# A written instruction order for the seven-product projections, and a later S5 gate, in a four-branch encoder layer

## The chip, the cores and the metric

One NeuronCore of a Trainium2 chip runs the whole kernel as one program. The metric is device microseconds of one execution. A NeuronCore has four compute engines with a queue each, which run their instructions strictly in the order of that queue: TensorE (PE, matrix products; its weight loads are shown apart as PEld), VectorE (DVE), ScalarE (ACT) and GpSimd (POOL). SyncE (SP) does no arithmetic here; it issues DMA transfers, also in order. Engines wait for one another by semaphores.

## The reference

One layer over 2048 tokens of width 1024, all in float32. The input is normalised, and one matrix `w_in` projects it to twelve pieces of 512 columns and to 4 x 1024 merge gates. Four branches read the pieces: an S5 state-space scan with a gated output (`out = z * sigmoid(z @ w_glu + b)`), retention, differential attention and a cross-attention into a memory of 256 tokens. Then

```python
a_out = s5_branch(ssm_u, ...) * jax.nn.silu(ssm_gate)     # branch 0
b_out = retention_branch(...) * jax.nn.silu(ret_gate)     # branch 1
c_out = diff_attn_branch(...) * jax.nn.silu(diff_gate)    # branch 2
m_out = memory_branch(...) * jax.nn.silu(mem_gate)        # branch 3
br = jnp.einsum('bsnc,ncd->bsnd', branches, w_branch[l])
gates = jax.nn.sigmoid(merge.reshape(bsz, seq, N_BRANCH, D_MODEL) + b_merge[l])
merged = jnp.sum(gates * br, axis=2)
x = x + jnp.einsum('bsd,de->bse', merged, w_out[l])
```

## The kernel before

The tokens are worked off in two blocks of 1024, one after the other. A float32 operand is split into a rounded part and a remainder, names ending in `h` (or `_h`) and `l` (or `_l`): ScalarE writes the rounded part with a cast, VectorE or GpSimd subtracts it from the operand for the remainder. Each product is then three matmuls (high with high, high with low, low with high), so that a product over four tiles of 128 input rows is twelve matmuls of 128 x 512. No remainder, no matmul: the first product over a tile waits for the slower of the two engines.

Four stages of each block matter here.

**Projections** (`projections`, with the class `Pair`). What is left of `w_in` when the branches have been served: the memory query, two gates and the merge gates. The first pair of column blocks (`first`) is done plainly, four groups of 24 matmuls: (column block 0, token half 1), (1, 1), (0, 0), (1, 0). Its weights are `p_r`, split into `p_h` and `p_l`. The 21 pairs that follow use a scheme of Strassen's kind: seven products (`product`, step 0 to 6) stand for eight. Their token operands are sums and differences of the normalised input's tiles: `t1`, `t2`, `t3`, `t4`, computed once in a block by four generators `x_mix`, one for each tile of 128 rows, on VectorE (temporaries `x_a`, `x_b`, `x_c`, `x_f`) and split to `x_t2h`, `x_t2l` and so on; `t1` overwrites the input's own tiles `xh`, `xl`. The weights' sums (`p_s`, and `p_r` in place) are made by `prepare`, which runs `LEAD` steps ahead of the product. `collect` adds the products up. Beside them run 16 scans of the S5 branch, each in seven pieces hung on steps (`side`).

**Merge** (`Merge.run`): 32 units of 24 matmuls, eight for each branch in the order 2, 1, 3, 0. A unit multiplies `br_h`, `br_l` (the branch's output, read back from DRAM as `w_r` and split) by a tile of `w_branch` (`w1h`, `w1l`). VectorE multiplies the result by the gate tile `mg_g`, which SP loads one unit ahead from `me_d` into a ring of three buffers, and GpSimd adds the product to `merged` (`mg`, line 1277).

**Memory branch and S5 gate** (`merge_output`): steps of the merge alternate with the memory branch, then with `s5_z` (loads `z_st`), `s5_zsplit` (splits them to `zh`, `zl`) and `s5_glu` (groups of matmuls `mm<-zh,...`, a tanh `g_t`, two VectorE products, a store to DRAM). Branch 0's merge units read those stores.

**Output** (`output`): `merged` is split into `w1h`, `w1l` tiles, multiplied by `w_out`, and the residual `x` (loaded as `mg_t`) is added.

The order of each queue before is that which the framework's scheduler made of the program text.

## Time and profile before

| | us |
|---|---|
| median of 3 runs | 3021.39 (3019.27 to 3024.44) |
| the profiled execution's own time | 3017.78 |
| its span in the trace | 3016.0 |
| TensorE busy | 2872.6 (95%) |
| VectorE busy | 1958.8 (65%) |
| ScalarE busy | 1336.7 (44%) |
| GpSimd busy | 1234.1 (41%) |

The span is the time from the first to the last instruction in the trace; 1.78 us of the execution's time lie around it. Busy shares are averages over stages that differ much. In the trace the first block's projections begin at about 675 us and its merge at about 1140; the second block's begin at about 2204 and 2668.

### The profile page before, as it was taken

How to read it: one execution, taken by the hardware profiler on the slowest of the kernel's cores; microseconds unless marked ns; L12 is line 12 of the kernel's file. 1: busy time of each engine (PE TensorE's matmuls, PEld its weight loads, DVE VectorE, ACT ScalarE, POOL GpSimd, SP SyncE). 2: the span in 40 equal slices, each digit the busy share in tenths (PEclk: the TensorE clock that was granted, in tenths of full speed). 3: DMA queues.
4: the chain of work that ended last, by engine and by line, in shares of the span. 5: the costliest groups of instructions: out<-in, count | busy, mean ns of one | idle time of the engine just before them, and what ended most of it. 6: DMA issues, size and time to landing. Idle time of an engine off the chain costs nothing. (4 is left out here: it accounts for less than half of the span.)

```text
span 3016.0 us, 43039 instructions
## 1 busy us (share of the span) xinstructions
PE 2872.6 (95%) x14258; PEld 2372.2 (79%) x14258; DVE 1958.8 (65%) x4622; ACT 1336.7 (44%) x3365; POOL 1234.1 (41%) x1157
## 2 busy tenths in 40 slices
PE   7888999998999999999999999999999999999999
PEld 6776777777888888777788878778878888887777
DVE  7785477766756645656543378888777666546654
ACT  4223355563343344423433357776743444444332
POOL 3443543324444443555132242332244444435660
PEclk9999999999999999999999999999999999999999
DMA  4433422223444336555521220220224444355552
GB/s 135 108 96 85 124 67 71 71 89 122 147 154 147 132 110 207 191 181 168 162 78 37 64 72 17 63 62 17 64 96 148 154 147 142 126 189 170 190 173 92
DMA packets 319645, 351.74 MB, mean 117 GB/s; under 512 B 26735, under 2 KB 238782, under 8 KB 319422
## 3 DMA queue, kind: packets, MB, share of 16 engines
q1 hardware_dynamic: 317118, 340.60, 35.9%
q0 software_dynamic: 2304, 8.39, 0.9%
q8 instruction: 112, 1.84, 0.3%
q14 instruction: 111, 0.91, 0.1%
HBM read 247.99 MB, written 100.93 MB: 116 GB/s over the span
## 5 line engine op out<-in xcount | busy, mean ns | idle before, releaser
L1305 POOL TENSOR_TENSOR p_l<-p_r,p_h 128x512 fp32r<-128x512 f32 x260 | 359.8, 1387 | 439.9 <-ACT p_h L1304 436.9
L74 PE MATMUL mm<-w5h,xh 128*128 128x512 f32 x1024 | 436.7, 426 | 5.5 <-ACT xh L588 2.7
L75 PE MATMUL mm<-w5l,xh 128*128 128x512 f32 x1024 | 406.8, 397 | 3.1 <-POOL w5l L454 3.0
L76 PE MATMUL mm<-w5h,xl 128*128 128x512 f32 x1024 | 408.9, 399 | 0.0
L138 POOL TENSOR_TENSOR rms_r<-rms_m,mhalf 128x1 f32<-128x1 f32 (+1 forms) x228 | 177.1, 778 | 498.9 <-DVE rms_m L136 428.4
L1304 ACT CAST p_h<-p_r 128x512 fp32r<-128x512 f32 x260 | 160.3, 621 | 365.7 <-DVE p_r L1318 109.4
L769 ACT ACTIVATE pr<-sc,nm 128x512 f32<-128x512 f32 (+3 forms) x320 | 200.4, 627 | 148.2 <-DVE nm L767 146.6
L76 PEld LDWEIGHTS mm<-w5h,xl 128*128 128x128 f32 x1024 | 194.8, 190 | 44.1 <-issue 0.4
L74 PEld LDWEIGHTS mm<-w5h,xh 128*128 128x128 f32 x1024 | 195.9, 191 | 36.1 <-ACT xh L588 3.1
L75 PEld LDWEIGHTS mm<-w5l,xh 128*128 128x128 f32 x1024 | 196.0, 191 | 31.8 <-POOL w5l L454 4.3
L75 PE MATMUL sc<-br_l,w1h 128*128 128x512 f32 x496 | 197.1, 397 | 7.6 <-DVE br_l L1223 7.6
L74 PE MATMUL sc<-br_h,w1h 128*128 128x512 f32 x496 | 200.3, 404 | 3.8 <-DVE mg_g L1276 3.6
L767 DVE TENSOR_REDUCE nm<-sc 128x1 f32<-128x512 f32 (+3 forms) x320 | 193.1, 604 | 9.0 <-PE sc L763 5.0
L76 PE MATMUL sc<-br_h,w1l 128*128 128x512 f32 x496 | 196.3, 396 | 0.0
L1277 POOL TENSOR_TENSOR mg<-mg,mg_g 128x512 f32<-128x512 f32 x96 | 142.0, 1483 | 88.4 <-DVE mg_g L1276 80.3
L817 PEld LDWEIGHTS o<-vt,at 128*128 128x128 f32 x1088 | 141.0, 191 | 38.3 <-ACT at L810 30.2
L817 PE MATMUL o<-vt,at 128*128 128x128 f32 x1088 | 150.9, 278 | 17.2 <-ACT at L810 17.1
L471 POOL TENSOR_TENSOR w1l<-w_r,w1h 128x512 fp32r<-128x512 f32 x86 | 119.4, 1402 | 114.2 <-ACT w1h L470 107.1
L454 POOL TENSOR_TENSOR w5l<-w_r,w5h 128x512 fp32r<-128x512 f32 x72 | 96.9, 1350 | 114.4 <-ACT w5h L453 79.6
L1343 PE MATMUL sc<-xl,p_h 128*128 128x512 f32 x336 | 131.3, 391 | 3.4 <-DVE xl L1378 3.4
L1343 PE MATMUL mm<-xh,p_h 128*128 128x512 f32 x336 | 133.7, 398 | 0.3 <-ACT p_t L1413 0.3
L1343 PE MATMUL sc<-xh,p_h 128*128 128x512 f32 x336 | 131.4, 391 | 1.0 <-ACT p_h L1304 0.5
(397 smaller groups left out, 7654.2 us busy)
## 6 DMA issues: line engine op xcount, KB each, us to landing
p_r<-in_w_in SPq DMA_DIRECT2D x88, 512.0 KB
w_r<-in_w_in SPq DMA_DIRECT2D x144, 256.0 KB
me_d<-p_t SPq DMA_DIRECT2D x128, 256.0 KB
mg_g<-me_d SPq DMA_DIRECT2D x64, 512.0 KB
s_m<-mats_d SPq DMA_DIRECT2D x32, 640.0 KB
w_r<-in_w_branch SPq DMA_DIRECT2D x64, 256.0 KB
w_r<-br SPq DMA_DIRECT2D x64, 256.0 KB
n_x<-in_x SPq DMA_DIRECT2D x16, 512.0 KB
```

The costliest lines, as they stand in the source:

```text
L74: PE.matmul(out, l[0], r[0], start=first, stop=False)
L75: PE.matmul(out, l[0], r[1], start=False, stop=False)
L76: PE.matmul(out, l[1], r[0], start=False, stop=last)
L138: G.tensor_tensor(r, m, mhalf[:, 0:n], op=ALU.pow)
L471: G.tensor_tensor(lo, raw, hi.bitcast(F32), op=ALU.subtract)
L767: V.tensor_reduce(nm, s[:, 0:n], axis=AX.X, op=ALU.max, negate=True)
L769: A.activation(e[:, 0:n], s[:, 0:n], AF.Exp, bias=nm, accum_out=self.zz[:, m, c:c + 1])
L817: PE.matmul(self.o[:, 0:128], self.at[c][:, q * 128:(q + 1) * 128], self.st["vts"][c][:, q, :], start=c == 0 and q == 0, stop=c * 4 + q == ...
L1277: G.tensor_tensor(dst, dst, t, op=ALU.add)
L1304: A.copy(hi, x)
L1305: G.tensor_tensor(lo, x, hi.bitcast(F32), op=ALU.subtract)
L1343: PE.matmul(o, l[:, k, :], r, start=first and k == 0 and q == 0, stop=k == 3 and q == 2, skip_group_check=True)
```

## The change

Four things are changed.

1. In `projections`, the instructions of TensorE, VectorE, ScalarE and GpSimd are taken in the order of the program text (`tc.manual_schedule`); SP is left out of that. `x_mix` hands back control at more places, and the text calls it in a written sequence: `t2` first, then `t3` and `t1`, and `t4` only in the first three steps of the products (`late`). The first two remainders of the plain pair are computed on VectorE in place of GpSimd. The first scan of the S5 branch loads its data at step 5 in place of step 1.
2. The loads of branch 2 for the merge are requested some steps before they are split.
3. In the merge, `mg_g` has four buffers in place of three, the branches' raw tiles have a pool of their own (`b_r`, four buffers; before, `w_r`, shared with the weights), and in units 16 to 31 the second token half is added to `merged` by VectorE in place of GpSimd. The S5 gate's tiles are asked for at merge step 7 of the last stage and its groups start at step 26 (before: at once, and step 20).
4. In `output`, the residual has a name and three buffers of its own (`mg_x`) and is loaded two units ahead.

```diff
     nc = tc.nc
     V, A, G, PE, DMA = nc.vector, nc.scalar, nc.gpsimd, nc.tensor, nc.sync
+    ORDERED = {x.engine for x in (V, A, G, PE)}
...
 
         def prefetch(self):
             self.pools.append(self.cx.enter_context(pool("mrga", side="right")))
             self.w0 = self.cx.enter_context(pool("w0", side="right"))
-            self.raw = self.raw_w(0)
 
...
-        def load(self, n, k):
+        def request(self, n, k):
+            raws = []
+            for hf in range(2):
+                if self.rp is None:
+                    raw = rawp.tile([128, 512], F32, name="w_r", bufs=4)
+                else:
+                    raw = self.rp.tile([128, 512], F32, name="b_r", bufs=4)
+                DMA.dma_start(out=raw, in_=br_d[n][self.b][k][:, hf * 512:hf * 512 + 512])
+                raws.append(raw)
+            return raws
+
+        def load(self, n, k, raws=None):
             hi, lo = self.pair()
+            raws = raws or self.request(n, k)
             for hf in range(2):
                 s_ = slice(hf * 512, hf * 512 + 512)
-                raw = rawp.tile([128, 512], F32, name="w_r", bufs=4)
-                DMA.dma_start(out=raw, in_=br_d[n][self.b][k][:, s_])
+                raw = raws[hf]
                 A.copy(hi[:, s_], raw)
                 V.tensor_tensor(lo[:, s_], raw, hi[:, s_].bitcast(F32), op=ALU.subtract)
             self.br[n, k] = hi, lo
...
             self.gp = self.gx.enter_context(pool("gates", side="right"))
+            self.rp = self.gx.enter_context(pool("brraw", side="right"))
             self.load(2, 3)
...
-                t = self.gp.tile([128, TB], F32, name="mg_g", bufs=3)
+                t = self.gp.tile([128, TB], F32, name="mg_g", bufs=4)
                 DMA.dma_start(out=t, in_=me_d[self.b][n][d])
...
-                        G.tensor_tensor(dst, dst, t, op=ALU.add)
+                        (V if hf and u >= 16 else G).tensor_tensor(dst, dst, t, op=ALU.add)
                     yield
...
-        def split(self, x):
+        def split(self, x, eng=G):
             hi = self.pw.tile([128, 4, 128], F32R, name="p_h", bufs=LEAD + 2)
             lo = self.pw.tile([128, 4, 128], F32R, name="p_l", bufs=LEAD + 2)
             A.copy(hi, x)
-            G.tensor_tensor(lo, x, hi.bitcast(F32), op=ALU.subtract)
+            eng.tensor_tensor(lo, x, hi.bitcast(F32), op=ALU.subtract)
             return hi, lo
...
             A.copy(d[0][:, k, :], t)
+            yield
             V.tensor_tensor(d[1][:, k, :], t, d[0][:, k, :].bitcast(F32), op=ALU.subtract)
+            yield
 
         t1 = raw(x0h, x0l, k, "x_a", 4)
         b12 = raw(x1h, x1l, k, "x_b", 4)
...
-        split(t2, xs["t2"])
-        yield
-        split(b12, xs["t3"])
-        yield
+        yield from split(t2, xs["t2"])
+        yield from split(b12, xs["t3"])
+        yield from split(t1, xs["t1"])
         t4 = raw(x0h, x0l, 4 + k, "x_c", 2)
         V.tensor_tensor(t4, t4, xs["t2"][0][:, k, :].bitcast(F32), op=ALU.subtract)
         V.tensor_tensor(t4, t4, xs["t2"][1][:, k, :].bitcast(F32), op=ALU.subtract)
-        split(t4, xs["t4"])
-        yield
-        split(t1, xs["t1"])
-        yield
+        yield from split(t4, xs["t4"])
...
               "22": (x1h[:, 4:8, :], x1l[:, 4:8, :]), "t1": (x1h[:, 0:4, :], x1l[:, 0:4, :])}
-        with pool("xs") as xsp, pool("pw") as pw, pool("pe") as pe:
+        with pool("xs") as xsp, pool("pw") as pw, pool("pe") as pe, tc.manual_schedule(engines=ORDERED):
...
-            with pool("xm", side="right") as xm:
-                for u, x in enumerate(pairs):
-                    x.pr = (pw, first.pr)[u % 2]
-                pairs[0].load()
-                ws = [[first.split(first.raw[kh][:, :, i, :]) for kh in range(2)] for i in range(2)]
-                mixes = [x_mix(b, k, xs, xm) for k in range(4)]
-                for q, (i, hf) in enumerate(((0, 1), (1, 1), (0, 0), (1, 0))):
-                    for x in mixes:
-                        next(x)
-                    if q == 2:
-                        for g in range(LEAD):
-                            prepare(g)
-                    o = ps_mm()
-                    drain(proj_tr(o, b, hf, ws[i]))
-                    t = pe.tile([128, 512], F32, name="p_t", bufs=7)
-                    first.sink(i, hf, o, t)
-            sx = ExitStack()
+            mx = ExitStack()
+            xm = mx.enter_context(pool("xm", side="right"))
+            for u, x in enumerate(pairs):
+                x.pr = (pw, first.pr)[u % 2]
+            pairs[0].load()
+            ws = [[first.split(first.raw[kh][:, :, i, :], G if i else V) for kh in range(2)] for i in range(2)]
+            mixes = [x_mix(b, k, xs, xm) for k in range(4)]
+
+            def plain(i, hf):
+                o = ps_mm()
+                drain(proj_tr(o, b, hf, ws[i]))
+                t = pe.tile([128, 512], F32, name="p_t", bufs=7)
+                first.sink(i, hf, o, t)
+
+            def step(*ks):
+                for k in ks:
+                    next(mixes[k])
+
+
+            step(0, 1, 0)
+            plain(0, 1)
+            step(2, 1)
+            plain(1, 1)
+            step(3, 2, 3)
+            step(0, 1, 0, 2, 1, 3, 2, 3)
+            plain(0, 0)
+            step(0, 1, 0, 2, 1, 3, 2, 3)
+            for g in range(LEAD):
+                prepare(g)
+            plain(1, 0)
+            late = {0: (0, 1, 0, 1), 1: (2, 2), 2: (3, 3)}
+            sx, sp = ExitStack(), []
             side = {}
...
                 gen = scan(j)
-                for at in (1, 7, 8, 9, 10, 11, 13):
+                for at in (1 if j else 5, 7, 8, 9, 10, 11, 13):
...
             n = len(steps)
             for g, (u, s) in enumerate(steps):
+                if g == 5:
+                    mx.close()
+                    sp.append(sx.enter_context(pool("s5a", side="right")))
                 prepare(g + LEAD)
                 pairs[u].product(s)
                 pairs[u].collect(s)
+                for k in late.get(g, ()):
+                    next(mixes[k])
                 for gen in side.get(g, []):
                     next(gen)
-                if g == n - 24:
+                if g == n - 26:
                     sx.close()
                     ux.close()
                     mg.prefetch()
-                if n - 24 <= g < n - 6 and (n - g) % 6 == 0:
-                    mg.load(2, (g - n + 24) // 6)
-                if g == n - 7:
+                if g in (n - 30, n - 24, n - 17):
+                    raws = mg.request(2, (g - n + 30) // 6)
+                if g in (n - 25, n - 18, n - 11):
+                    mg.load(2, (g - n + 25) // 7, raws)
+                if g == n - 10:
+                    mg.raw = mg.raw_w(0)
+                if g == n - 5:
                     mg.first()
...
+        xrs = {}
+
+        def residual(i):
+            if i < len(units):
+                eh, t = units[i]
+                xrs[i] = gp.tile([128, 512], F32, name="mg_x", bufs=3)
+                r0 = b * TB + t * 128
+                DMA.dma_start(out=xrs[i], in_=a["x"][0][r0:r0 + 128, eh * 512:(eh + 1) * 512])
+
+        for i in range(2):
+            residual(i)
...
-            xr = gp.tile([128, 512], F32, name="mg_t", bufs=5)
+            residual(i + 2)
+            xr = xrs.pop(i)
             r0 = b * TB + t * 128
-            DMA.dma_start(out=xr, in_=a["x"][0][r0:r0 + 128, eh * 512:(eh + 1) * 512])
...
-            ob = gp.tile([128, 512], F32, name="mg_t", bufs=5)
+            ob = gp.tile([128, 512], F32, name="mg_t", bufs=2)
...
         with pool("s5b") as sp:
-            z = s5_z(b, sp)
-            zsplit = s5_zsplit(z)
             ws = {}
-            glus = chain_of(s5_glu(b, e, mg.w1, sp, z, ws) for e in range(4))
             for q in range(128 - MEM_STEPS + 64):
                 next(merge)
-                if q == 12:
+                if q == 7:
+                    z = s5_z(b, sp)
+                    zsplit = s5_zsplit(z)
+                    glus = chain_of(s5_glu(b, e, mg.w1, sp, z, ws) for e in range(4))
+                if q == 18:
                     ws[0] = s5_wg(mg.w1, 0)
-                if 4 <= q < 20 and q % 2 == 0:
+                if 10 <= q < 26 and q % 2 == 0:
                     next(zsplit)
-                if q >= 20:
+                if q >= 26:
                     next(glus, None)
             drain(glus)
```

What this does to the queues is shown at three places; the first rows of each pair are of before, the second of the kernel after the change. Numbers behind names tell tiles of one name apart.

VectorE at the start of block 0's projections, behind the last norm of the attention branch (`rms_m`), before:

```order
L136 TENSOR_SCALAR rms_m_8132<-ho_ss_8130 128x1
L1373 TENSOR_TENSOR x_a_8266<-xh_302,xl_303 128x512
L1373 TENSOR_TENSOR x_b_8268<-xh_529,xl_530 128x512
L1373 TENSOR_TENSOR x_c_8270<-xh_529,xl_530 128x512
L1384 TENSOR_TENSOR x_a_8266<-x_b_8268,x_a_8266 128x512
L1373 TENSOR_TENSOR x_a_8278<-xh_302,xl_303 128x512
L1385 TENSOR_TENSOR x_f_8272<-x_c_8270,x_a_8266 128x512
L1386 TENSOR_TENSOR x_b_8268<-x_c_8270,x_b_8268 128x512
L1373 TENSOR_TENSOR x_b_8280<-xh_529,xl_530 128x512
```

and after:

```order
L137 TENSOR_SCALAR rms_m_8132<-ho_ss_8130 128x1
L1317 TENSOR_TENSOR p_l_8253<-p_r_8146,p_h_8252 128x512
L1317 TENSOR_TENSOR p_l_8257<-p_r_8148,p_h_8256 128x512
L1385 TENSOR_TENSOR x_a_8268<-xh_302,xl_303 128x512
L1385 TENSOR_TENSOR x_b_8270<-xh_529,xl_530 128x512
L1385 TENSOR_TENSOR x_c_8272<-xh_529,xl_530 128x512
L1398 TENSOR_TENSOR x_a_8268<-x_b_8270,x_a_8268 128x512
L1399 TENSOR_TENSOR x_f_8274<-x_c_8272,x_a_8268 128x512
L1400 TENSOR_TENSOR x_b_8270<-x_c_8272,x_b_8270 128x512
```

The two remainders `p_l` now stand in front of the mixing, and the mixing of tile 0 comes whole before that of tile 1.

ScalarE at the same place, from the evacuation of the S5 input (`us`) on; `p_t` is the copy of a plain group's result out of its bank. Before:

```order
L985 COPY us_8162<-mm_8189 128x64x8
L1413 COPY p_t_8339<-mm_8314 128x512
L1377 CAST xh_529<-x_a_8266 128x512
L1377 CAST x_t2h_8241<-x_f_8272 128x512
L1377 CAST x_t2h_8241<-x_f_8284 128x512
L1377 CAST x_t3h_8239<-x_b_8268 128x512
```

and after:

```order
L986 COPY us_8162<-mm_8189 128x64x8
L1389 CAST x_t2h_8243<-x_f_8274 128x512
L1389 CAST x_t2h_8243<-x_f_8285 128x512
L1423 COPY p_t_8316<-mm_8291 128x512
L1389 CAST x_t2h_8243<-x_f_8325 128x512
L1423 COPY p_t_8356<-mm_8331 128x512
L1389 CAST x_t2h_8243<-x_f_8365 128x512
L1389 CAST x_t3h_8241<-x_b_8270 128x512
```

The third and the fourth cast to `x_t2h` now stand behind the copies of the first and the second plain group.

SP in the S5 gate stage of block 0, around the first stores of branch 0 (`br0`), before:

```order
L1081 DMA g_g_13697<-ag_d0_1_161 128x512
L1221 DMA w_r_13883<-br0_0_0_83 128x512
L1093 DMA br0_0_0_83<-g_t_13683 128x512
L1081 DMA g_g_13740<-ag_d0_1_161 128x512
L1247 DMA mg_g_13801<-me_d0_3_4_196 128x1024
L1221 DMA w_r_13887<-br0_0_0_83 128x512
```

and after:

```order
L1259 DMA mg_g_13856<-me_d0_3_5_197 128x1024
L1094 DMA br0_0_0_83<-g_t_13677 128x512
L1082 DMA g_g_13735<-ag_d0_1_161 128x512
L1223 DMA b_r_13860<-br0_0_0_83 128x512
L462 DMA w_r_14044<-in_w_branch 128x4x128
L1094 DMA br0_0_0_83<-g_t_13720 128x512
L1082 DMA g_g_13778<-ag_d0_1_161 128x512
L1223 DMA b_r_13862<-br0_0_0_83 128x512
```

The gate tile that is loaded next (`me_d0_3_4`, branch 3, column tile 4) stood between two loads of branch 0; now the tile behind it (`me_d0_3_5`) has been loaded before the first store of that branch.

## Rows read from the trace of the kernel before

**Rows 1.** The page: busy us of each engine, share of the span, instructions.

```profile
PE 2872.6 (95%) x14258; PEld 2372.2 (79%) x14258; DVE 1958.8 (65%) x4622; ACT 1336.7 (44%) x3365; POOL 1234.1 (41%) x1157
```

**Rows 2.** TensorE's waits, whole span: who released it, us, times, longest.

```profile
PE sc L75 <- DVE br_l L1223: 7.6, 2, 3.8
PE mm L74 <- ACT g_t L1088: 6.8, 2, 4.2
...
PE sc L1343 <- ACT p_h L1304: 4.1, 2, 3.6
PE mm L74 <- DVE mg_t L1539: 3.7, 2, 2.4
PE sc L74 <- DVE mg_g L1276: 3.6, 2, 1.8
...
PE sc L1343 <- DVE xl L1378: 3.4, 2, 2.6
PE mm L76 <- POOL p_l L1305: 3.3, 1, 3.3
PE sc L74 <- ACT br_h L1222: 3.3, 3, 1.7
PE mm L76 <- POOL w1l L471: 3.1, 4, 1.5
...
PE sc L1343 <- POOL p_l L1305: 1.8, 1, 1.8
```

**Rows 3.** Windows: us, PE, PEld, DVE, ACT, POOL busy, granted clock, DMA share, GB/s.

```profile
675.00:700.00 25.00, 21.71 (x88) 17.41 (x88) 14.44 (x24) 12.23 (x21) 12.43 (x5) 0.93 0.41 127
700.00:725.00 25.00, 19.60 (x70) 15.13 (x69) 20.15 (x33) 8.37 (x16) 8.40 (x6) 0.80 0.18 63
...
1315.00:1340.00 25.00, 20.79 (x84) 16.50 (x83) 16.76 (x16) 5.46 (x9) 13.38 (x9) 0.93 0.52 168
1365.00:1390.00 25.00, 23.17 (x95) 18.68 (x94) 13.48 (x18) 5.85 (x17) 18.70 (x15) 0.93 0.56 177
```

**Rows 4.** Groups by line, TensorE, 740 to 1130 us: busy, mean ns, idle before.

```profile
L1343 PE MATMUL sc<-xh,p_h 128*128 128x512 f32 x156 | 60.7, 389 | 0.0
```

**Rows 5.** Two matmuls a product of twelve apart (start, us).

```profile
726.39 0.39 PE L1343 MATMUL sc<-x_t3h,p_h 128*128 128x512 f32 x1
...
729.11 0.39 PE L1343 MATMUL mm<-xh,p_h 128*128 128x512 f32 x1
```

**Rows 6.** Block 0's start: line L1305 from 676 us (ns, min/median/max), timelines DVE, POOL.

```profile
L1305 POOL TENSOR_TENSOR p_l<-p_r,p_h x5: 1276/1282/7467, 678.2 to 689.4; 128x512 fp32r<-128x512 f32 x5
...
683.90 0.69 DVE L1373 TENSOR_TENSOR x_b<-xh,xl 128x512 f32<-128x512 f32 x1
...
715.32 3.40 POOL L1305 TENSOR_TENSOR p_l<-p_r,p_h 128x512 fp32r<-128x512 f32 x1 [24.65 <-ACT p_h L1304]
...
716.92 0.68 DVE L1315 TENSOR_TENSOR p_s<-p_r 128x512 f32<-128x512 f32 x1
```

**Rows 7.** Block 1's start: timelines of ACT, POOL and DVE.

```profile
2215.70 1.09 ACT L985 COPY us<-mm 128x512 f32<-128x512 f32 x1 [1.47 <-PE mm L76]
...
2233.64 5.85 POOL L1305 TENSOR_TENSOR p_l<-p_s,p_h 128x512 fp32r<-128x512 f32 x1 [6.69 <-ACT p_h L1304]
...
2257.97 0.69 DVE L1315 TENSOR_TENSOR p_s<-p_r 128x512 f32<-128x512 f32 x1 [4.05 <-DMA p_r<-in_w_in]
```

**Rows 8.** S5 gate stage, block 0: timelines of SP and ACT.

```profile
1264.89 8.29 ACT L1064 ACTIVATE zh<-z_st 128x1024 fp32r<-128x1024 f32 x4 [8.46 <-DMA z_st<-z_d]
...
1320.14 0.32 SPq L1247 DMA_DIRECT2D mg_g<-me_d  x1
...
1324.67 0.62 ACT L1222 CAST br_h<-w_r 128x512 fp32r<-128x512 f32 x1 [7.46 <-DMA w_r<-br]
```

**Rows 9.** End of the merge and output projection, block 0: timeline of DVE.

```profile
1372.04 5.83 DVE L1526 SCALAR_TENSOR_TENSOR w1l<-mg,w1h 128x128 fp32r<-128x128 f32 x3 [2.78 <-ACT w1h L1525]
...
1400.12 9.82 DVE L1526 SCALAR_TENSOR_TENSOR w1l<-mg,w1h 128x128 fp32r<-128x128 f32 x10
```

## What I expect

> **What bounds the kernel now.** I read the page first. TensorE is busy for 95% of the span [rows 1], so what the change can give back lies in the stretches where TensorE stands, or runs at the lower of its two clock levels (1.2 in place of 2.4 GHz). The waits of TensorE by releaser, over the whole span, say which of these the change can reach [rows 2]. The start of the projections: 3.6 us for a cast `p_h` and 3.3 and 1.8 us for remainders `p_l` in block 0, 3.4 us for `xl` and 0.5 us (4.1 less 3.6) for `p_h` in block 1, where the reader should see VectorE and GpSimd as the late engines. The start of the merge: 3.1 of the 3.3 us at `br_h`, once in each block (the third, 0.2 us, belongs to the gate stage). The S5 gate stage: 7.6 us for `br_l` (3.8 the longer), 6.8 us for `g_t` (4.2) and 1.5 us for a weight's remainder `w1l`. The merge's end: 3.6 us for `mg_g`, 1.8 in each block. The output: 3.7 us for `mg_t`.
>
> Then the windows, for the clock [rows 3]. Between 700 and 725 us the granted clock was 0.80 on the mean, so 0.20 x 25 = 5.0 us were lost to it; between 675 and 700, between 1315 and 1340 and between 1365 and 1390 it was 0.93, 1.75 us each. Each stands at or behind one of the waits above. In all that is 38.9 us of waits and 10.25 of clock: 1.6% of the time is the most that these edits can win. Between the starts and the ends of the projections nothing is to be won: the products there have no idle time in front of them [rows 4], and a product of twelve matmuls takes 2.72 us, from one row of [rows 5] to the other.
>
> **The projections' start, block 0.** Here lies the question of the change. GpSimd's first remainder took 7.47 us against 1.28 for the median of the same instruction [rows 6]. It started at 678.24, while VectorE ran sums of two tiles in SBUF without a gap, and ended at 685.71; the last of VectorE's run had started at 683.90 and taken 0.69, so it ended 1.1 us before. The remainder at 715.32 took 3.40 and ended at 718.72, again 1.1 us behind the end of VectorE's run at 716.92 + 0.68. In block 1 one took 5.85 [rows 7]. So GpSimd makes no progress until VectorE stops; then it needs 1.1 us.
>
> After the change VectorE does the first two remainders itself, and column block 0 no longer waits: 3.3 us less. But then come 24 mixing operations and three remainders `x_t2l` in the written order, and no one of them has cause to wait: the casts they need stand behind `us` and the copy of the first plain group only. VectorE's pace is 20.15 / 33 = 0.61 us [rows 3], so the run of 29 lasts 17.7 us, from 678.2 to 695.9. The fourth `x_t2l` stands behind the copy of the second plain group, and VectorE must stop. GpSimd, which has the two remainders of column block 1, finishes the first at 697.0. When would TensorE want it? Before, it wanted column block 0's at 682.4 (685.71 less 3.3); a plain group is two products, 5.44 us, so the second group wants its own at 687.8. That is a wait of 9.2 us.
>
> Behind it, step 1's remainder: the six operations of `t4` (3.7 us) stand right behind the sum that step 1 needs, so GpSimd ends 3.7 + 1.1 = 4.8 us behind that sum. The sum itself overwrites what step 0's remainder reads, so it ends some 0.7 us after that remainder; TensorE, released by it, wants step 1's after one product and a bit, 3 us. That leaves 0.7 + 4.8 - 3.0 = 2.5 us of waiting. Sum for block 0: before 8.7 of waits and 6.75 of clock, after 11.7 and, at one stretch of 1.75 behind each wait, 3.5. Gain 0.3 us. Bounds: a loss of 3.0 if the clock falls behind one of the two for as long as it did between 700 and 725; a gain of 15.4 if GpSimd isn't held up at all.
>
> **The rule that bears on this.** The Trainium skill, SBUF — State Buffer, section Who interferes with whom, says that a VectorE instruction with two SBUF inputs contends with a GpSimd instruction that reads SBUF, that the pair of ports is an exclusive lock held for the whole instruction, and that issue order decides who blocks. [Rows 6] agree that GpSimd is blocked. But read literally the lock is free at each end of a VectorE instruction, so that GpSimd would get in 0.6 us later; by that the wait of 9.2 us is none (the first rival below), by the rows it stands. The rows decide here.
>
> **Block 1.** Here ScalarE comes late with `us` (2215.70 + 1.09 [rows 7]), because TensorE does, and the first cast `x_t2h` stands behind it. VectorE has run through two remainders and twelve sums by about 2215 (14 x 0.61 from 2206.4) and stands for some 2.5 us, enough for both of GpSimd's remainders at 1.28. The waits of 3.9 us go, step 1's 2.5 come: gain 1.4, the clock alike. Bounds 0 and 5.
>
> **Merge start.** `br_h` stands on ScalarE behind a cast that waits for a load of the memory branch. That load is now issued ahead of one gate tile, not behind it. I take 1.0 of the 3.1 us; bounds 0 and 3.1.
>
> **S5 gate.** The first stall (7.6 us in both blocks) I leave as it is: `br_h` still stands behind four `zh`, 8.29 us in a row [rows 8]. Their loads now stand behind a load that waits for a store, which could cost 3 us a block; the later start of the gate's matmuls could give 1 back. The `w1l` wait goes, since the gate's first weights are loaded ahead: 1.5. The `g_t` waits: SP stood until 1320.14 to issue a gate tile, for want of a buffer in a ring of three, and the load of the branch behind it came so late that ScalarE's cast, in front of `g_t`, ran at 1324.67 after 7.46 idle. With four buffers and the raw tile's own pool SP doesn't stand for the ring and waits for the store's landing alone. I take 6.0 of 6.8 us, and 1.75 of clock. Together 9.25; bounds 1 and 10.
>
> **Merge end.** GpSimd was busy for 18.7 of 25 us [rows 3], and VectorE, in order, stood 2.78 us for a `w1h` that waits for GpSimd's sums, then took 5.83 for three groups of splits [rows 9], with TensorE's `mg_g` behind. Half of the sums move: about four in 25 us, 5.1 us of GpSimd against 2.4 on VectorE, which had only 13.5. I take 4.0 of 3.6 + 1.75; bounds -1 and 5.35.
>
> **Output.** The residual wasn't what TensorE waited for: VectorE's adds were, behind splits of 0.98 us each (9.82 for ten [rows 9]). Loading the residual earlier gives nothing; GpSimd's shorter backlog gives some. I take 1.5 of 3.7; bounds -1 and 3.7.
>
> **Written order in the steady products.** It can only lose. Casts and remainders are prepared four products ahead (10.9 us), so most has slack; for the S5 scans' bank behind `collect` I take off 1.5. Bounds 0 and, below, the slower rival.
>
> **Sum.** 0.3 + 1.4 + 1.0 + 9.25 + 4.0 + 1.5 - 1.5 = 15.95. The profiled execution would take 3017.8 - 16.0 = 3001.8; it ran 3.6 us below the median, and against that I predict 3021.4 - 16 = 3005.4 us.
>
> **Rivals.** First, GpSimd gets in between VectorE's instructions: the 9.2 us, both 2.5 and two stretches of 1.75 go, 17.7 us more: 2987.7. For it: in block 1 the five remainders had a median of 1.74. Against: three that were held to the end. Chance 0.10. Second, the relief of GpSimd does nothing at the merge's end and in the output: 5.5 less, 3010.9. For it: VectorE gets 32 more operations in a stage where it stood in order. Chance 0.13. Third, as the second, and the gate's first stall grows by 3 us a block: the waits are only moved, 3016.9. Chance 0.20. Fourth, slower: VectorE's fixed order stalls the products. Its place is `p_s`, which waits for the load `p_r` once for each of 42 pairs, with the products' collection behind it; in block 1 it stood 4.05 us there [rows 7], harmless only because the scheduler put it where nothing was urgent. From 16 / 42 = 0.38 us a pair on, the gain is eaten; at 0.7 us the time is 3034.8. Against it: 10.9 us of lead. Chance 0.12.
>
> **How the numbers follow.** My forecast keeps 0.45: 3005.4, by its own bounds 2999 to 3011. A difference under 0.2%, 6 us, can hardly be told from none. Faster: the forecast, the first two rivals and a quarter of the third, 0.73; same: most of the third, 0.14; slower: the fourth and a bit, 0.13. The range 2989 to 3020 leaves out the slower rival and what lies beyond the first.
>
> **What would show it.** At the start of block 0, a TensorE wait of about 9 us on `p_l` in the second plain group with a GpSimd instruction of 15 us or more beside it; if that instruction takes under 3, the first rival holds. Behind it 2.5 us in step 1 of both blocks. In the gate stage no wait on `g_t` over 1 us, and SP's gate tile loads without a wait; at the merge's end no wait on `mg_g`. Any idle time of TensorE in the steady products shows the fourth rival. I am wrong if the start loses more than I think, or if the gate's first stall grows beyond 7 us.

## The result and the profile after

| | us |
|---|---|
| before, median of 4 runs | 3020.61 (3019.27 to 3024.44) |
| after, median of 4 runs | 3004.80 (3001.02 to 3008.16) |
| ratio | 0.9945, 95% interval 0.9927 to 0.9963 |
| profiled execution after | 3007.83, span 3005.9 |

The change gave 15.8 us by the medians, and 0.55% by the ratio; the prediction's sum was 15.95. The two profiled executions lie only 9.95 us apart (3017.78 and 3007.83), because before's ran below its median and after's above.

The waits of TensorE over the whole span of the changed kernel, which answer to [rows 2] (who released it, us, times, longest):

```profile
PE sc L75 <- ACT br_h L1233: 7.4, 4, 2.3
PE sc L76 <- DVE br_l L1234: 6.5, 2, 3.3
...
PE sc L1355 <- DVE p_t L1364: 4.9, 2, 2.4
...
PE sc L1355 <- DVE p_t L1367: 4.1, 2, 2.3
PE sc L75 <- DVE mg_g L1288: 3.8, 4, 1.3
PE mm L75 <- DVE mg_t L1583: 3.6, 2, 3.2
...
PE sc L1355 <- POOL p_l L1317: 1.6, 2, 0.8
PE mm L1355 <- POOL p_l L1317: 1.4, 1, 1.4
PE mm L77 <- POOL w1l L472: 1.3, 2, 0.6
```

`g_t` is gone (6.8 before) and `w1l` has fallen from 3.1 to 1.3. `br_h` with `br_l` has grown from 10.9 to 13.9; the first stall's part of it is 7.8 before (2 x 3.8 and 0.2) and 11.1 after (the 6.5 of `br_l`, and 2.3 of `br_h` in each block). `mg_g` stands at 3.8 for 3.6, but elsewhere: none at the merge's end, 1.3 and 0.9 us at the memory branch's part of the merge and 0.9 and 0.7 at the first stall. In the memory branch's part TensorE stood before for a tile of that branch, at the same matmuls:

```profile
PE sc L74 <- ACT m_pr L1144: 2.1, 2, 1.1
```

At the projections' start `p_h`, `xl` and `p_l` stood for 4.1 + 3.4 + 3.3 + 1.8 = 12.6 us; now 4.9 + 4.1 + 1.6 + 1.4 = 12.0 stand there, on other tiles: `p_t`, the sum that collects a product's result, is new.

The windows of [rows 3], the third of them the gate's first stall, and the last the merge's end:

```profile
675.00:700.00 25.00, 25.00 (x112) 20.68 (x111) 21.88 (x33) 10.41 (x18) 3.07 (x2) 1.00 0.45 138
700.00:725.00 25.00, 20.33 (x80) 15.72 (x79) 23.17 (x27) 9.51 (x19) 12.29 (x7) 0.93 0.13 43
1260.00:1285.00 25.00, 18.50 (x69) 14.18 (x68) 19.53 (x35) 11.64 (x11) 15.36 (x8) 0.86 0.65 210
1315.00:1340.00 25.00, 25.00 (x110) 20.42 (x109) 19.69 (x21) 6.31 (x11) 14.47 (x9) 1.00 0.66 207
1365.00:1390.00 25.00, 25.00 (x112) 20.71 (x111) 13.99 (x31) 6.93 (x25) 8.59 (x7) 1.00 0.13 44
```

Before, the third of them was:

```profile
1260.00:1285.00 25.00, 19.47 (x78) 15.09 (x77) 19.29 (x42) 12.76 (x12) 13.85 (x8) 0.93 0.63 206
```

The granted clock is the figure behind POOL's. Before, it was 0.93 and 0.80 in the first two windows and 0.93 in the last two. In the first and the last two TensorE is now busy for the whole 25 us and holds 2.4 GHz; the second still loses some, and the gate's first stall loses more than before (0.86 for 0.93). GpSimd is busy 8.59 us at the merge's end where it was 18.70.

If the same TensorE instruction, by its number in the order, is looked up in both traces, its shift says where time was won. Sums over both blocks, us:

| term | predicted | found in the profiled pair |
|---|---|---|
| projections' start, block 0 | +0.3 | +5.0 |
| projections' start, block 1 | +1.4 | -1.7 |
| steady products | -1.5 | 0 |
| merge start and the gate's first stall | +1.0 | -4.7 |
| `g_t`, `w1l`, with the clock | +9.25 | +8.8 |
| merge end | +4.0 | +5.8 |
| output | +1.5 | -0.2 |
| elsewhere, by difference (2.5 of it in the next block's first stage) | 0 | -3.05 |
| sum | 15.95 | 9.95 |

The total was right by luck: three of the seven terms were 3 to 6 us off, in both directions, and in run 1 below the same two kernels lie 21.8 us apart by the medians. The loss in the next block's first stage stands at a stretch that the change doesn't touch: the same longest wait of 2.3 us in both traces, and a clock of 0.80 behind it after (1485 to 1510 us) for 0.93 before (1495 to 1520). Repeated runs of one kernel differ by as much.

### The profile page after: what moved, and what is told of

It reads as the page before. It is cut to its first block, busy times and chain, and to the rows that moved or that the text cites. A ratio compares the mean times of both kernels' runs of the same rounds, so it can differ in the third digit from the quotient of the medians.

```text
span 3005.9 us, 42936 instructions
## 1 busy us (share of the span) xinstructions
PE 2873.4 (96%) x14258; PEld 2374.6 (79%) x14258; DVE 1944.0 (65%) x4658; ACT 1315.7 (44%) x3365; POOL 1176.3 (39%) x1121
## 5 line engine op out<-in xcount | busy, mean ns | idle before, releaser
L1317 POOL TENSOR_TENSOR p_l<-p_r,p_h 128x512 fp32r<-128x512 f32 x256 | 348.5, 1368 | 495.4 <-ACT p_h L1316 493.6
L1289 POOL TENSOR_TENSOR mg<-mg,mg_g 128x512 f32<-128x512 f32 x64 | 96.3, 1508 | 119.0 <-DVE mg_g L1288 95.5
L1438 ACT ACTIVATE p_t<-p_t,vec 128x512 f32<-128x512 f32 x96 | 69.5, 724 | 157.8 <-DVE p_t L1367 75.7
```

The source lines that it names most:

```text
L1317: eng.tensor_tensor(lo, x, hi.bitcast(F32), op=ALU.subtract)
```

## Experiments

Each ratio is that to the kernel before, measured beside it on the same chip, with its 95% interval. Where two of these kernels lie within 4 us of each other, their time alone doesn't tell them apart, and the rows must.

**1. The changed kernel again.** No edit.

> The changed kernel once more, for its interval and a second trace. Both theories: about 3004.8 us, 0.995 of before. What the second trace can tell: if the start of block 0 has the same waits (1.6 and 0.95 us on p_l, 2.6 and 2.0 us on p_t) they belong to the program; if the granted clock falls at other places than in the first trace (0.80 in the 25 us behind the start of the next block's work), the spread of 7 us between runs is the clock's.

2999.39 us (2992.82 to 3006.23), ratio 0.9929 (0.9911 to 0.9947). The profiled run shows the same waits at the products' start, 2.4, 1.8, 1.4 and 0.8 us. So the waits are the kernel's own, and a median moves by some 5 us from one measurement to the next.

**2. and 3. Halves of the change.** Run 2 has the new projections and early requests with the old merge, gate and output; run 3 the old projections with all the rest of the change.

```diff
# run 2: against the changed kernel
-            self.rp = self.gx.enter_context(pool("brraw", side="right"))
-                t = self.gp.tile([128, TB], F32, name="mg_g", bufs=4)
+                t = self.gp.tile([128, TB], F32, name="mg_g", bufs=3)
-                        (V if hf and u >= 16 else G).tensor_tensor(dst, dst, t, op=ALU.add)
+                        G.tensor_tensor(dst, dst, t, op=ALU.add)
...
# run 3: class Pair, x_mix and projections as before the change
```

> Only the written order in the projections and the earlier requests for branch 2's loads; merge, S5 gate and output as before. The sum on record gives the starts 0.3 + 1.4 and takes 1.5 off: 0.2 us faster than before, 3020.4. The rival, read from the trace after: 5.0 us faster at block 0's start, 1.7 slower at block 1's: 3.3 us faster, 3017.3. In both the waits on g_t (6.8 us) and mg_g (3.6 us) are there again.

> The projections as before, in the scheduler's order; merge, S5 gate and output as in the change. The sum on record gives 9.25 + 4.0 + 1.5: 14.75 us faster, 3005.9. Read from the trace after, with the first gate stall longer and the output of block 0 slower: 10.7 us faster, 3009.9. If the parts add up, this and the run with the order alone give the whole gain of 15.8.

Run 2: 3016.64 us (3011.8 to 3021.5), ratio 0.9987 (0.9977 to 0.9997). Run 3: 3004.20 us (3001.82 to 3008.89), ratio 0.9945 (0.9929 to 0.9961). Before stood at 3021.18 beside them, so the written order is worth some 4 us and the merge some 17. The prediction's own split was 0.3 + 1.4 - 1.5 = 0.2 and, with the 1.0 of the merge start, 15.75. In run 3 the old order again holds GpSimd's first remainder for over 7 us; five of them on line L1318, ns, min, median and max:

```profile
L1318 POOL TENSOR_TENSOR p_l<-p_r,p_h x5: 1282/1287/7449, 679.8 to 690.9; 128x512 fp32r<-128x512 f32 x5
```

**4. All four first remainders on GpSimd**, in the new order.

```diff
-... first.split(first.raw[kh][:, :, i, :], G if i else V) ...
+... first.split(first.raw[kh][:, :, i, :], G) ...
```

> The changed kernel with all four remainders of the plain pair on GpSimd again (before: two on VectorE). Theory A (on record: GpSimd makes no progress until VectorE's run of sums ends): VectorE mixes from 673 on without a gap for some 16 us, GpSimd's first remainder starts at 678 and ends some 1.1 us behind the first gap, about 690, and TensorE waits about 8 us in the first plain group: 3013. Theory B (GpSimd gets in between VectorE's instructions, 1.7 us a remainder, as in the trace after): the first remainder ends about 680, no wait, 3004.

3001.57 us (2992.21 to 3004.61), ratio 0.9929 (0.9912 to 0.9946), that of the changed kernel. Its timelines of GpSimd and VectorE:

```profile
678.23 6.70 POOL L1317 TENSOR_TENSOR p_l<-p_r,p_h 128x512 fp32r<-128x512 f32 x4 [4.08 <-ACT p_h L1316]
...
678.00 0.68 DVE L1385 TENSOR_TENSOR x_c<-xh,xl 128x512 f32<-128x512 f32 x1
678.61 1.79 DVE L1398 TENSOR_TENSOR x_a<-x_b,x_a 128x512 f32<-128x512 f32 x1
680.50 1.59 DVE L1399 TENSOR_TENSOR x_f<-x_c,x_a 128x512 f32<-128x512 f32 x1
```

GpSimd asks at 678.23, as it did at 678.24 in [rows 6], with VectorE mixing at its 0.60 us pace both times. Before, it was held until 685.71. Here four remainders are through in 6.70 us, and it is VectorE whose instructions take 1.79 in place of 0.68. So GpSimd is freed without moving two remainders to VectorE: at this place the order in which VectorE mixes does it. Whether the move would do it alone, with the old order, no run shows.

**5. Two lines of the mixing exchanged.** In the order before, VectorE's instructions start 0.60 us apart; in the new one `x_f` stands right behind the `x_a` that it reads, and starts 0.71 behind it. The edit parts the two.

```diff
-        V.tensor_tensor(t2, b22, t1, op=ALU.subtract)
         V.tensor_tensor(b12, b22, b12, op=ALU.subtract)
+        V.tensor_tensor(t2, b22, t1, op=ALU.subtract)
```

> The changed kernel with two adjacent independent lines of the mixing exchanged, so that the second subtraction of a tile no longer stands directly behind the one whose result it reads. Theory A (GpSimd gets at memory where VectorE has to wait for its own last result, 0.71 us from start to start in place of 0.60): with no such neighbours left at the first mixing, GpSimd's two first remainders in block 0 take 7.4 us together again as before the change, in place of 3.07, TensorE waits 8 to 9 us for them, and the time is about 3009. Theory B (it is the place where the remainders stand against the run of VectorE, or VectorE's waits for ScalarE's casts, that lets GpSimd in): 3 to 4 us for the pair, no wait over 1.5 us on p_l, and the time of the changed kernel, 3000 to 3005.

3001.64 us (2998.36 to 3006.21), ratio 0.9937 (0.9923 to 0.9952); the pair of first remainders took 3.07. That looks like theory B, but the edit didn't do what it says. VectorE's timeline:

```profile
684.39 0.68 DVE L1398 TENSOR_TENSOR x_a<-x_b,x_a 128x512 f32<-128x512 f32 x1
685.10 0.69 DVE L1399 TENSOR_TENSOR x_b<-x_c,x_b 128x512 f32<-128x512 f32 x1
```

`x_b` now stands behind the `x_a` that still reads it, and the 0.71 us is there again. The run decides nothing; run 12 does it properly.

**6. The early remainders on VectorE**, eleven in each block.

```diff
-                self.w[0] = self.split(a11)
+                self.w[0] = self.split(a11, self.eng)
...
+            pairs[0].eng = V
-... first.split(first.raw[kh][:, :, i, :], G if i else V) ...
+... first.split(first.raw[kh][:, :, i, :], V) ...
```

> The changed kernel with all four first remainders and the seven remainders of the first pair of products moved from GpSimd to VectorE. Theory A (the waits at the products' start, p_t 2.4 and 2.3, 1.8, and p_l 1.4 and 0.8, about 4.5 us in a block, come from GpSimd and VectorE working by turns at 1.7 us an instruction): without GpSimd's instructions there VectorE keeps its 0.60 us pitch, the waits on p_t and p_l at the first three products go, and the time falls by 5 to 8 us to about 2995. Theory B (VectorE has simply too much to do there, the mixing of t4 standing ahead of the collects): seven more instructions of some 0.4 us make the collects as late or later, p_t waits of 2 us or more stay, time 3000 to 3006.

2997.84 us (2997.43 to 2999.01), ratio 0.9923 (0.9910 to 0.9937). The waits on `p_l` are gone, but not those on `p_t`:

```profile
PE sc L1355 <- DVE p_t L1364: 6.5, 2, 3.5
...
PE sc L1355 <- DVE p_t L1367: 2.8, 2, 2.3
```

9.3 us in place of 9.0. The collects are late without VectorE's lengthened instructions too: six sums and two splits of `t4` stand in front of the first of them. VectorE has nine remainders more in each block than in the changed kernel, though, so what the turns alone cost there isn't told apart. Theory B; the 3.0 us of `p_l` are what the rows show as won.

**7. ScalarE in written order in the first 26 steps of merge and gate.**

```diff
+            with tc.manual_schedule(engines={A.engine}):
+                for q in range(26):
+                    turn(q)
+            for q in range(26, 128 - MEM_STEPS + 64):
+                turn(q)
```

> The changed kernel with ScalarE held to the written order in the first 26 steps of the stage where merge and gate interleave, so that the casts of the memory branch's tiles go ahead of all four casts of the scan's output. Theory A (the first stall, 7.4 on br_h and 6.5 on br_l over both blocks, is a ScalarE cast that was put behind a cast which waits for the scan's output): both rows go or shrink under 1 us a block, and the time falls by 8 to 12 us to about 2992. Theory B (TensorE only meets the stall later: the scan's output is late whatever ScalarE does, and the gate's products then wait for z_l or g_t): the br rows go, but waits of about the same sum stand in the gate; 2999 to 3005.

3000.92 us (2998.87 to 3003.96), ratio 0.9933 (0.9921 to 0.9946): no gain. TensorE's waits:

```profile
PE mm L76 <- DVE zl L1067: 6.4, 4, 2.5
...
PE sc L75 <- DVE mg_g L1288: 5.4, 3, 3.2
...
PE sc L77 <- POOL w1l L472: 2.9, 1, 2.9
...
PE sc L75 <- ACT br_h L1233: 2.0, 2, 1.2
```

`br_l` is gone and `br_h` down to 2.0, as theory A has it; but 6.4 us on `zl`, more on `mg_g` and a new `w1l` of 2.9 take their place. Whichever of the two groups of casts goes first, TensorE meets the other. Theory B.

**8. The gate's steps put back**, with the rest of the change kept.

```diff
+            z = s5_z(b, sp)
+            zsplit = s5_zsplit(z)
+            glus = chain_of(s5_glu(b, e, mg.w1, sp, z, ws) for e in range(4))
...
-                if q == 18:
+                if q == 12:
-                if 10 <= q < 26 and q % 2 == 0:
+                if 4 <= q < 20 and q % 2 == 0:
-                if q >= 26:
+                if q >= 20:
```

> The changed kernel with the gate's part of the merge stage put back to its earlier steps (scan's output at once, its weights at step 12, its units from step 20). Theory A (the shift itself removed the waits on g_t, 6.0 us over both blocks, and paid for it with some 2 us a block of a longer first stall): g_t waits of about 6 us and w1l of 1 to 1.5 return, the br rows fall by 3 to 4 us, and the time is 2 to 5 us above the changed kernel, 3004 to 3008. Theory B (the deeper ring of mg_g and the additions moved to VectorE removed those waits): no g_t wait, shorter first stall, 2997 to 3000.

2995.35 us (2993.74 to 2999.71), ratio 0.9917 (0.9903 to 0.9930), the best median so far. No wait on `g_t` came back, and the first stall is short again:

```profile
PE sc L76 <- DVE br_l L1234: 6.0, 2, 3.1
...
PE sc L75 <- ACT br_h L1233: 4.1, 4, 1.6
```

10.1 us in place of 13.9, of which the first stall has 8.1 for 11.1. The later gate did not remove the waits on `g_t`, it only lengthened the stall ahead of them: theory B.

**9. Both: runs 6 and 8 together.**

> The changed kernel with the gate's steps put back (as in the eighth run) and the early remainders on VectorE (as in the sixth). Theory A (the two act at different places, the start of the products and the first stall of the merge, so what they give adds up): br rows of about 10 us over both blocks in place of 13.9, no wait on p_l, and 2990 to 2994. Theory B (what the remainders gave is only where the clock fell, since p_t waits of 9.3 us stand there with or without them): the eighth run's 2995 to 2998.

2995.29 us (2993.67 to 2998.35), ratio 0.9913 (0.9900 to 0.9926). It beats the kernel before by 0.9%; against run 8 it is no gain that the time shows, though its waits on `p_t` and `p_l` come to 9.4 us and run 8's to 4.9 + 3.7 + 1.6 + 1.4 = 11.6.

**10. and 11. Run 9 without the buffers, and run 9 without the moved sums.**

```diff
# run 10
-            self.rp = self.gx.enter_context(pool("brraw", side="right"))
-... name="mg_g", bufs=4)
+... name="mg_g", bufs=3)
# run 11
-                        (V if hf and u >= 16 else G).tensor_tensor(dst, dst, t, op=ALU.add)
+                        G.tensor_tensor(dst, dst, t, op=ALU.add)
```

> The ninth run's kernel without the deeper buffers of the merge (mg_g three in place of four, no buffers of its own for the memory branch's raw halves). Theory A (these buffers took away the waits on g_t and w1l, 9.9 us before the change): g_t waits of 5 to 7 us and w1l of 2 to 3 are back and the time is 6 to 9 us above the ninth run, about 3000. Theory B (the additions moved to VectorE did it): no g_t wait and the time of the ninth run, within 2 us.

> The ninth run's kernel with all additions of the merge back on GpSimd. Theory A (the additions moved in the last units took away the waits on mg_g at the merge's end, about 1.8 us a block and a half-speed stretch of the clock): mg_g waits of 3 to 4 us are back, and the time is 4 to 6 us above the ninth run. Theory B (the fourth buffer of mg_g took them away): no such waits, the time of the ninth run within 2 us. If the additions also took away the g_t waits, those are back too, and the time is some 10 us above.

Run 10: 2999.29 us (2994.65 to 3003.02), ratio 0.9924 (0.9912 to 0.9936). Run 11: 2998.86 us (2991.32 to 3000.58), ratio 0.9920 (0.9907 to 0.9933). Both intervals overlap that of run 9, so the rows decide. TensorE waits on `g_t` for 1.5 us in run 9, 0.5 in run 10 with three buffers, and in run 11, with the sums on GpSimd:

```profile
PE mm L75 <- ACT g_t L1089: 4.7, 4, 2.3
```

So it is the sums. How, the timelines of GpSimd, SP and ScalarE of run 11 show:

```profile
1311.16 2.13 POOL L1289 TENSOR_TENSOR mg<-mg,mg_g 128x512 f32<-128x512 f32 x1
...
1313.32 0.32 SPq L1259 DMA_DIRECT2D mg_g<-me_d  x1
...
1317.84 0.62 ACT L1233 CAST br_h<-b_r 128x512 fp32r<-128x512 f32 x1 [7.42 <-DMA b_r<-br]
```

GpSimd's sum ends at 1313.29 and gives a buffer back; at 1313.32 SP issues the gate tile that waited for it, and behind it the load `b_r`; ScalarE, in order, stands 7.42 us for `b_r` with `g_t` behind. In run 9 VectorE's sum gives the buffer back, and SP goes on 5.2 us sooner (ScalarE stands for a `b_r` there too, 8.49 us, but its `g_t` starts at 1315.66 in place of 1318.88):

```profile
1307.39 0.68 DVE L1289 TENSOR_TENSOR mg<-mg,mg_g 128x512 f32<-128x512 f32 x1
...
1308.09 0.32 SPq L1259 DMA_DIRECT2D mg_g<-me_d  x1
```

At the merge's end no wait on `mg_g` came back in either run: there the buffers alone or the sums alone seem to be enough, and neither theory as written holds. No run has the rest of the change without both, so something that both runs keep, such as the residual's earlier loads, isn't ruled out. What run 10 lost by its rows is 1.1 us of `w1l` (2.4 for 1.3); whether its 4 us are real stays open.

**12. The old mixing order, written out**, on the kernel of run 4.

```diff
         t1 = raw(x0h, x0l, k, "x_a", 4)
+        yield
...
         V.tensor_tensor(t1, b12, t1, op=ALU.subtract)
+        yield
...
-            step(0, 1, 0)
+            step(0, 0, 1, 0, 1, 2, 1, 0)
-            step(2, 1)
+            step(2, 3, 2, 1)
-            step(3, 2, 3)
+            step(3, 3, 2, 3)
```

> The fourth run's kernel (all four first remainders on GpSimd) with the written mixing order at the first three tiles changed to that of before, where one tile's load stands between two instructions of which the second reads the first's result, so that VectorE's run has no start-to-start distance over 0.61 us. Theory A (GpSimd gets in where VectorE has no further instruction ready behind the next one): GpSimd's first remainder takes 4 to 7.5 us at a run of VectorE at 0.60 us, TensorE waits some us for p_l at the first plain groups, and the time is 3 to 9 us above the fourth run. Theory B (something else in the changed kernel lets it in): first remainders of 1.6 to 1.8 us each, time of the fourth run, about 3000.

2999.10 us (2993.21 to 3004.93), ratio 0.9925 (0.9909 to 0.9940). Line L1317 on GpSimd (ns, min, median and max) and VectorE's timeline:

```profile
L1317 POOL TENSOR_TENSOR p_l<-p_r,p_h x4: 1293/1516/3867, 679.2 to 685.5; 128x512 fp32r<-128x512 f32 x4
...
678.84 0.68 DVE L1385 TENSOR_TENSOR x_c<-xh,xl 128x512 f32<-128x512 f32 x1
679.44 0.69 DVE L1399 TENSOR_TENSOR x_a<-x_b,x_a 128x512 f32<-128x512 f32 x1
680.04 0.68 DVE L1385 TENSOR_TENSOR x_a<-xh,xl 128x512 f32<-128x512 f32 x1
680.65 0.68 DVE L1401 TENSOR_TENSOR x_f<-x_c,x_a 128x512 f32<-128x512 f32 x1
681.25 0.68 DVE L1402 TENSOR_TENSOR x_b<-x_c,x_b 128x512 f32<-128x512 f32 x1
684.60 1.53 DVE L1391 TENSOR_TENSOR x_t2l<-x_f,x_t2h 128x512 fp32r<-128x512 f32 x1 [2.67 <-ACT x_t2h L1389]
```

GpSimd asks at 679.21, again in an `x_c`, again with the `x_a` that reads `x_b` next. In run 4 it got in ahead of that `x_a`, whose follower `x_f` reads what it writes. Here an independent load follows, and VectorE ran on at 0.60 us until it stood for ScalarE's cast; the remainder ended at 679.21 + 3.87 = 683.08, 1.15 us behind the last of the run. In block 1 the two runs part likewise: the first remainder took 2.74 us in run 12, ending 1.15 us behind VectorE's run, and 1.30 in run 4. For this pair of runs the mechanism of theory A holds, not its time: VectorE's stop came in time for TensorE.

## Why the prediction was right in its sum, and where it was not

**The wait of 9.2 us in block 0's second plain group: wrong, and the prediction's first rival had the mechanism.** The step that failed is "GpSimd makes no progress until VectorE stops". In the changed kernel it gets in by turns; its two remainders, and VectorE's instructions beside them:

```profile
678.98 3.07 POOL L1317 TENSOR_TENSOR p_l<-p_r,p_h 128x512 fp32r<-128x512 f32 x2 [5.08 <-ACT p_h L1316]
...
679.12 1.78 DVE L1385 TENSOR_TENSOR x_a<-xh,xl 128x512 f32<-128x512 f32 x1
680.83 1.78 DVE L1385 TENSOR_TENSOR x_b<-xh,xl 128x512 f32<-128x512 f32 x1
```

I drew the rule from three instances in an order that the change replaces, and read the third wrongly. In block 1's 5.85 us VectorE did not stop; GpSimd was let in ahead of an `x_t4l`, and the two went by turns from there on. Timelines of VectorE and GpSimd before:

```profile
2237.66 2.38 DVE L1378 TENSOR_TENSOR x_t4l<-x_c,x_t4h 128x512 fp32r<-128x512 f32 x2
2239.97 3.47 DVE L1373 TENSOR_TENSOR x_c<-xh,xl 128x512 f32<-128x512 f32 x2
...
2239.45 5.13 POOL L1305 TENSOR_TENSOR p_l<-p_r,p_h 128x512 fp32r<-128x512 f32 x3
```

So both manners stood in the trace that I predicted from. Nor did VectorE have to stop at the fourth `x_t2l`, as I said: in the changed kernel it followed the third at the usual pace (two in 1.29 us from 697.54). The forecast's own test, a GpSimd instruction of 15 us or one under 3, came out at 1.4 and 1.7.

**The rival's time was wrong as well**, for it left out the price of turns. At the first products VectorE mixes `t4` beside GpSimd's remainders (both timelines of the changed kernel):

```profile
709.14 1.74 POOL L1317 TENSOR_TENSOR p_l<-p_s,p_h 128x512 fp32r<-128x512 f32 x1
...
708.08 1.65 DVE L1406 TENSOR_TENSOR x_c<-x_c,x_t2l 128x512 f32<-128x512 f32 x1
709.65 1.78 DVE L1385 TENSOR_TENSOR x_c<-xh,xl 128x512 f32<-128x512 f32 x1
711.47 1.66 DVE L1405 TENSOR_TENSOR x_c<-x_c,x_t2h 128x512 f32<-128x512 f32 x1
```

and the collects `p_t` stand behind that mixing: 4.9 + 4.1 us over both blocks, which no term of mine had. Run 6 shows that VectorE has too much there without the turns as well, though not what the turns add. In block 0 the gain of 5.0 is 8.7 - (2.4 + 1.8 + 1.4 + 0.8) = 2.3 us of waits, and I put the other 2.7 down to the clock. The first two windows lost 6.75 us to it before and 1.75 after, more than 2.7, but part of that fell into waits, where it costs nothing: from 714.5 to 724.5 us before, at a clock of 0.50, TensorE was busy for only 7.38 of the 10. In block 1 the other 12.0 - 6.4 = 5.6 us stand where 3.9 stood. Step 1's own wait was 0.8 in both blocks, not 2.5.

**The gate: the size was right (8.8 for 9.25), the reasons were not.** For `g_t` I named the four buffers and the raw tiles' own pool. Runs 10 and 11 show that the sums moved to VectorE did it, by giving the same ring back sooner: SP still waits for the ring. I had counted those sums at the merge's end alone. For `w1l` I named the weights' earlier loading; it is gone with the old steps too (run 8), and 0.9 us of it is back at the gate without the buffers (run 10).

**The gate's first stall** was to stay at 7.6 for `br_l`, with a warning that it could cost 3 us a block. It cost 11.1 - 7.8 = 3.3 us over both, and 1.6 of `mg_g` beside. ScalarE's timeline in the changed kernel:

```profile
1265.96 6.04 ACT L1065 ACTIVATE zh<-z_st 128x1024 fp32r<-128x1024 f32 x3
1271.80 2.18 ACT L1233 CAST br_h<-b_r 128x512 fp32r<-128x512 f32 x4
```

The memory branch's casts still stand behind those of `zh`, as I said. Run 8 shows nearly all of it to be the moved steps (8.1 with the old ones). At the merge's start `br_h` fell only from 3.1 to 2.8, and behind it 2.2 us for `mg_g` stand where 2.1 for `m_pr` stood.

**Merge end: right** (4.0 forecast, 5.8 found, clock back at 1.00). That runs 10 and 11 each keep it suggests two remedies for one stall; it isn't shown.

**Output: wrong in block 0.** GpSimd's backlog was shorter, but the last of VectorE's splits ended only 11.1 us sooner (1398.80 for 1409.94), where TensorE was 12.3 ahead by then; VectorE's timeline:

```profile
1389.69 9.11 DVE L1570 SCALAR_TENSOR_TENSOR w1l<-mg,w1h 128x128 fp32r<-128x128 f32 x12
...
1400.90 0.68 DVE L1583 TENSOR_TENSOR mg_t<-mm,mg_x 128x512 f32<-128x512 f32 x1
```

Twelve in 9.11 us where ten took 9.82, and TensorE still stands 3.2 us for the sum behind them. In block 1 it won 2.1, which I can't tell from where the clock fell.

**The fourth rival**, a stall in the steady products, didn't come about.

## What to carry to other kernels

Of two engines that read the same memory, look at the order of the faster one's instructions before moving work between them: here one order held GpSimd for 7.5 us and another let it in at once, for the price of 1.1 us to VectorE each time; in that order, moving two instructions to the other engine made no difference that the time shows. When an in-order queue stands for a free buffer, ask who gives the buffer back and when: the earlier sum did here what a fourth buffer was meant to do. And split a change with several edits: the later gate, which cost some 3 us of waits in each execution and bought none, was hidden in a sum that came out right.

## What the runs showed of the hardware that I had not expected

VectorE and GpSimd, each reading two tiles in SBUF, held each other up in one of two manners. Under VectorE's gapless run GpSimd got nowhere: 7.47 and 7.45 us (before and run 3), 3.87 (run 12), each ending 1.1 to 1.2 us behind the run, where one takes 1.28 alone. In the other manner both go by turns, some 1.7 us for a pair of instructions, 6.70 for four (run 4). The Trainium skill, SBUF — State Buffer, section Who interferes with whom, has an exclusive lock for the whole of an instruction, and the issue order decides. Run 4 agrees, but by that GpSimd would have got in behind one VectorE instruction of 0.68 us in run 12 as well, and five went first. What separated runs 4 and 12 in VectorE's queue was whether an instruction that doesn't need the next one's result stands behind it.

Other places don't follow from that. In the changed kernel the remainder at 702.92 took 2.45 us and let one instruction more pass than run 4 would suggest. The one at 678.98 got in ahead of the `x_a` at 679.12, although the `x_b` behind it reads nothing of that `x_a`: in run 9, with no GpSimd beside them, the two start at 680.73 and 681.33, the usual 0.60 apart. So the condition is shown for the pair of runs alone, and its inner cause stays open. Since `x_a` and `x_b` open the mixing in the old order too, the two remainders moved in front of them may have freed GpSimd in the changed kernel whatever order follows.

A wait taken from TensorE was worth about twice its length where the clock fell behind it. In the window from 1365 to 1390 us, 1.83 us of idle TensorE (25.00 less 23.17 busy [rows 3]) went together with a clock of 0.93, another 1.75 us; without the wait the clock was 1.00. The same wait in block 1, 1.8 us, cost no clock:

```profile
2900.00:2925.00 25.00, 23.15 (x101) 18.67 (x100) 16.31 (x30) 6.94 (x25) 14.90 (x13) 1.00 0.22 73
```

By the shifts of TensorE's instructions the merge's end won 3.7 us in block 0 and 2.1 in block 1.
